# A two-layer decoder trunk: the first and last pairs of tiles of each feed-forward reordered, operands queued among products, and the mixer's last heads beside its first outputs

## The chip, the cores and the metric

The kernel runs on one core of one Trainium2 chip. The metric is device time in microseconds (us); three runs of the kernel before are shown.

## The reference, cut to what matters

Two layers, 512 positions, width 1024, everything in fp32. `ada` is an RMS norm whose scale and shift, like the gates, come from a linear map of `silu(c)`.

```
mod = silu(c) @ w_ada[layer] + b_ada[layer]          # (3 sub-blocks, shift/scale/gate, 1024)
x = x + 0.5 * gate0 * swiglu(ada(x, 0), w1[layer, 0], w2[layer, 0])
x = x + gate1 * mixer(ada(x, 1))                     # q|k|v heads + short conv, then @ w_out
x = x + 0.5 * gate2 * swiglu(ada(x, 2), w1[layer, 1], w2[layer, 1])
# swiglu(h): g, up = split(h @ w1); (silu(g) * up) @ w2, inner width 2816
# mixer: 8 heads of 64, a causal softmax over keys at three dilations; conv: gb * conv3(gc * u)
```

## The kernel before, in words

**Products.** Each fp32 product is three passes of TensorE (PE) over operands that are split into a high and a low half: high by high, high by low, low by high (`product` L273 to L275, `shared_bulk` L280). A weight tile of 128 by 1024 that has landed in `raw`, `left` or `sum` is split by `halves`: ScalarE (ACT) writes `whi` (L167), VectorE (DVE) writes `wlo` (L168). The activations are kept split as `h`.

**Order of the work.** A layer is a feed-forward (FFN), the mixer, and a second FFN; so there are four FFNs and two mixers. The order of all weight units is written out by `_units`, and inside an FFN by `_ffn_order`. `weights` takes them in that order; `fetch` loads them some units ahead (SyncE's queue, SP) and splits them two ahead (`AHEAD`).

**The FFN's first product** is made with seven products of half-size blocks in place of eight. Its 2816 inner columns are 11 pairs of tiles, n = 0 to 10; each pair has seven units of 24 matmuls (128x256), called n.1 to n.7 below. Unit 1 is block b11 in a `left` tile (three buffers). Unit 2 is b12 and unit 4 is b22, in `raw` tiles (five buffers). Unit 5 is b21 + b22 in a `sum` tile (two buffers): SP loads b21, and a GpSimd (POOL) accumulate-DMA adds b22 to it (`add_block`, L179). Unit 6 is that `sum` with b11 taken off (L218), unit 7 is `left` after another accumulate-DMA of b21, which is issued after L218. Unit 3 is b12 less the sum (L221), after which the `sum` buffer is free for the next pair but one. The moving operands of units 1 and 2 are made by `Blocks.early`, those of the others by `t1` to `t4`. After units 7 and 3, `evacuation` makes the hidden tiles `hidh`, `hidl` from the banks.

**The second product** is made in three parts (`PARTS`: pairs 0 to 3, 4 to 7, 8 to 10), P0 and P1 among the units, P2 at the end. `Tail.run` makes one: for each of eight output tiles j, one unit of w2 and its matmuls of 128x512, then the addition into `x` (L526). In P2 the first two j run `side_by_side`, with the last two of their products after the others, and the last three j are run in two halves of 256 columns, so that the norm behind them can start on the first half.

**Queued steps.** `after(columns, step)` puts a step on a list that `tick` works off as PE's products go by; `flush` runs what is left at once. The modulations of later sub-blocks are jobs (`later`: one 128x1024 multiply-and-sum on DVE, L299, after a load of 512 KB); `next_job` gives them out after units 7 and 3 and between the j of P0 and P1. The kernel before gives 61, 26, 52 and 0 of them to the four FFNs.

**The mixer** makes four groups of heads and four groups of convolution, `MIXER`; the attention steps of a group (`attend`: transposes of p L807, products with v L816) are queued among the products of the next. At the end the last group's steps are flushed, the eight y are split into a new `h`, and `Tail.run` makes the output product.

Of the kernel before, what the change touches and what calls it, by code (L numbers as in the profile page):

```python
# [19 lines left out]
S = 512  # L20
# [20 lines left out]
LATER = 2048  # L41

# [44 lines left out]
def _ffn_order():  # L87


    order = [[(0, 1), (0, 2)], [(1, 1), (1, 2)], [(2, 1)], [(2, 2)]]  # L90
    order += [[u] for u in ((0, 5), (1, 5), (0, 6), (1, 6), (0, 7), (2, 5), (0, 4), (0, 3), (1, 7), (2, 6), (1, 4),
                            (1, 3), (3, 1), (2, 7), (3, 2), (2, 4), (2, 3))]
    ends = [p0 + n - 1 for p0, n in PARTS]
    for n in range(3, NP):
        order += [[(n, 5)], [(n, 6)]]
        if n - 1 in ends:
            order += [[("part", ends.index(n - 1))]]
        for p, q in ((1, 7), (2, 4)):
            if n + 1 < NP:
                order += [[(n + 1, p)]]  # L100
            order += [[(n, q)]]
        order += [[(n, 3)]]
    return order + [[("part", len(PARTS) - 1)]]
# [3 lines left out]
def trunk(ctx: ExitStack, tc: tile.TileContext, t: dict):  # L107
# [16 lines left out]
    def half_kb(name):  # L124
        return tmp.tile([128, S], F32, name=name, tag="ev", bufs=7)
# [209 lines left out]
    def later(l, s):  # L335
# [177 lines left out]
    class Tail:  # L513
# [18 lines left out]
        def run(self, ks, key, done, pool=None, side_by_side=0):  # L532
# [4 lines left out]
            n = len(ks)  # L537
# [13 lines left out]
            if side_by_side:  # L551
                banks = [acc_bank() for _ in range(2)]
                for j in range(2):
                    ws[j] = weights(*key, j)
                    products(banks[j], j, slice(0, S), range(n - side_by_side))
                for j in range(2):
                    products(banks[j], j, slice(0, S), range(n - side_by_side, n))
                    self.add(j, banks[j], slice(0, S), done)
                j0 = 2
            for j in range(j0, full):  # L560
                ws[j] = weights(*key, j)
                part(j, slice(0, S))
                if not done:
                    next_job(2)
# [16 lines left out]
            def change(half, rb):  # L581
                for j in range(KD):
                    modulate(h, self.nl, self.ns, rb, HALVES[half], j)

            r = None
            for cols in HALVES:
# [4 lines left out]
                if r:  # L591
                    flush()
                    if blocks:
                        for k in range(KD // 2):
                            blocks.early(r[1], k)
                    else:
                        change(0, r[1])
                r = norm(cols)
            if blocks:
# [6 lines left out]
            elif not self.last:  # L606
                after(0, lambda: change(1, r[1]))
# [80 lines left out]
    def ffn(l, s, h, carried, groups=()):  # L688
# [16 lines left out]
        for at, group in enumerate(todo):  # L705
            if group[0][0] != "part":
                feed(l, which, h, group, banks, done)
                if group[0][1] in (7, 3):

                    left = len(jobs) - 2 * KD * sum(g[0][0] == "part" and g[0][1] < len(PARTS) - 1 for g in todo[at:])  # L710
# [18 lines left out]
    def mixer(l, s, h):  # L729
# [13 lines left out]
        with tc.tile_pool(name="mix", bufs=1) as mp:  # L743
            y = {}

            def project(g):

                ws = [weights("qkv", l, g, u) for u in range(4)]
                qk, v = [], []
                for pair in ((0, 1), (2, 3)):  # L750
                    if g == 0 and pair[0]:
                        flush()
                    banks = [acc_bank()[:, :384] for _ in pair]
                    for k in range(KD):
                        o = (k % 2) * 384
                        for b, ps in zip(pair, banks):
                            tb = slice(b * 128, (b + 1) * 128)
                            bulk(ps, (hh[k][:, tb], hl[k][:, tb]), [w[:, o:o + 384] for w in ws[k // 2]],
                                 k == 0, k == KD - 1)
                    ss = tmp.tile([128, 8], F32, name="sm", tag="sm", bufs=24)  # L760
                    raw = []
                    for i, ps in enumerate(banks):
                        sq = mp.tile([128, 256], F32, name="qq", tag="qq", bufs=2)
                        nc.scalar.activation(sq, ps[:, 0:256], AF.Square)
                        nc.vector.reduce_sum(ss[:, 4 * i:4 * i + 4], sq.rearrange("p (a h) -> p a h", h=HD), axis=AX.X)

                        vt = spare_part("v", 256).rearrange("p (i m h) -> p i m h", i=2, m=2)
                        split(vt[:, :, 0], vt[:, :, 1], ps[:, 256:384].rearrange("p (i h) -> p i h", h=HD))
                        v.append(vt)
                        qn = mp.tile([128, 256], F32, name="qn", tag="qn", bufs=3).rearrange("p (a h) -> p a h", h=HD)  # L770
                        nc.vector.tensor_tensor(out=qn, in0=ps[:, 0:256].rearrange("p (a h) -> p a h", h=HD),
                                                in1=qkg[:, l], op=ALU.mult)
                        raw.append(qn)
                    r = rsqrt(ss, 8, 1.0 / HD)
                    for i, qn in enumerate(raw):
                        nc.vector.tensor_tensor(out=qn, in0=qn, op=ALU.mult,
                                                in1=r[:, 4 * i:4 * i + 4, None].to_broadcast([128, 4, HD]))

                        qt = mp.tile([128, 6, 2, HD], F32R, name="qk", tag="qk", bufs=4)
                        split(qt[:, 0:2, 0], qt[:, 0:2, 1], qn[:, 0:2])  # L780
                        split(qt[:, 2:4], qt[:, 4:6], qn[:, 2:4, None, :].to_broadcast([128, 2, 2, HD]))
                        qk.append(qt)
                return qk, v

            def attend(g, qk, v):

                y[g] = mp.tile([128, S], F32, name="ya", tag="y", bufs=8)
                stacks = [[None] * 3 for _ in range(2)]
                probs, moved = {}, {}

                def lift(i, n):
                    stacks[i][n] = stack(qk, i + 2 * n)

                def soften(b, i):
                    probs[b, i] = softmax(b, stacks[i])

                def turn(b, i):
                    half = b // 2
                    if b % 2 == 0:

                        moved[half, i] = [mp.tile([128, 4, 256], F32R, name=n, tag=n, bufs=2) for n in ("ph", "pl")]
                        for z in moved[half, i]:
                            nc.gpsimd.memset(z[:, 2 * half + 1, 0:128].bitcast(F32), 0.0)
                    p = probs.pop((b, i))
                    pt = tp_bank()
# [238 lines left out]
```

## Time and the profile before

| | |
|---|---|
| median of three runs | 1974.92 us (1971.2 to 1977.33) |
| profiled execution | 1973.8 us, its span 1971.7 us |
| mean granted TensorE clock | 0.976 |
| PE busy | 1864.1 us, 95% |
| PEld (weight loads) busy | 1724.1 us, 87% |
| DVE busy | 1441.7 us, 73% |
| ACT busy | 948.0 us, 48% |
| POOL busy | 88.5 us, 4% |

The profiled execution lies 1.1 us below the median. A clock of 1.0 stands for 2.4 GHz and 0.5 for 1.2 GHz; 0.976 is a mean over the span. Matmuls overlap, so what tells most is PE's idle time and what ended it.

### The profile page before, as it was taken

Reading aid. Unit: us, or ns where it says so; the run is one execution under the profiler, and the core shown is the slowest. Engines: PE = TensorE matmul, PEld = TensorE weight load, DVE = VectorE, ACT = ScalarE, POOL = GpSimd, SP = SyncE. Lnnn points to the kernel's source line nnn. Section 1 sums busy time; section 2 is a strip of 40 time slices with the busy share of each in tenths; the row PEclk is TensorE's granted clock in tenths of the full one; section 3 lists DMA queues with packets and bytes.
Section 4 is the critical chain, followed back from the end, with each engine's and each line's share of the span. In section 5 each row is a group of like instructions: output and inputs, shape, how many; then the busy total and the mean of one; then the engine's idle time right before and its main releaser. Section 6 shows DMA issues by size and latency. Waiting matters only on the chain. (4 is left out here: it accounts for less than half of the span.)

```text
span 1971.7 us, 31053 instructions
## 1 busy us (share of the span) xinstructions
PE 1864.1 (95%) x12340; PEld 1724.1 (87%) x12340; DVE 1441.7 (73%) x2458; ACT 948.0 (48%) x1483; POOL 88.5 (4%) x164
## 2 busy tenths in 40 slices
PE   4899899999999799999988999999999998999998
PEld 3798898899978798998887989898898798989898
DVE  7897878787865777775677878786977767747563
ACT  4552543446653562543464536343655654536342
POOL 0100000000000000000000000000000000000000
PEclk9899999999999899999998999999999998999999
DMA  8778776421314368674507777843222407626422
GB/s 332 185 236 271 209 234 211 142 81 60 108 65 128 70 168 255 180 206 145 152 23 192 234 247 203 273 122 98 81 70 97 143 18 171 167 85 165 131 57 83
DMA packets 86277, 300.52 MB, mean 152 GB/s; under 512 B 9458, under 2 KB 10482, under 8 KB 86132
## 3 DMA queue, kind: packets, MB, share of 16 engines
q1 hardware_dynamic: 73460, 252.40, 37.4%
q0 software_dynamic: 12672, 46.14, 13.8%
q8 instruction: 97, 1.59, 0.3%
q14 instruction: 48, 0.39, 0.1%
HBM read 296.41 MB, written 2.10 MB: 151 GB/s over the span
## 5 line engine op out<-in xcount | busy, mean ns | idle before, releaser
L280 PE MATMUL acc<-h,whi 128*128 128x256 f32 x4928 | 912.0, 287 | 49.0 <-ACT whi L167 22.6
L280 PEld LDWEIGHTS acc<-h,whi 128*128 128x128 f32 x4928 | 783.7, 195 | 58.0 <-ACT whi L167 24.7
L280 PE MATMUL acc<-h,wlo 128*128 128x256 f32 x2464 | 705.2, 287 | 14.9 <-DVE wlo L168 14.9
L280 PEld LDWEIGHTS acc<-h,wlo 128*128 128x128 f32 x2464 | 479.6, 195 | 18.5 <-DVE wlo L168 18.5
L167 ACT ACTIVATE whi<-raw 128x1024 fp32r<-128x1024 f32 (+1 forms) x300 | 302.9, 1012 | 387.0 <-PE acc L274 227.0
L168 DVE TENSOR_TENSOR wlo<-raw,whi 128x1024 fp32r<-128x1024 f32 (+1 forms) x300 | 347.7, 1164 | 60.2 <-ACT whi L167 56.6
L273 PE MATMUL acc<-hidh,whi 128*128 128x512 f32 (+1 forms) x776 | 287.4, 370 | 10.6 <-ACT whi L167 10.6
L274 PE MATMUL acc<-hidl,whi 128*128 128x512 f32 (+1 forms) x776 | 287.3, 370 | 0.0
L275 PE MATMUL acc<-hidh,wlo 128*128 128x512 f32 (+1 forms) x776 | 287.0, 370 | 0.0
L299 DVE SCALAR_TENSOR_TENSOR ada<-ada,cb 128x1024 f32<-128x1024 f32 x144 | 174.4, 1222 | 72.6 <-DMA ada<-in_w_ada 72.2
L526 DVE SCALAR_TENSOR_TENSOR x<-acc,fin,x 128x512 f32<-128x512 f32 (+1 forms) x130 | 87.7, 675 | 143.4 <-PE acc L275 143.0
L167 ACT ACTIVATE whi<-sum 128x1024 fp32r<-128x1024 f32 x88 | 93.3, 1060 | 177.4 <-DVE sum L218 99.2
L273 PEld LDWEIGHTS acc<-hidh,whi 128*128 128x128 f32 x776 | 146.2, 188 | 35.6 <-ACT whi L167 11.4
L274 PEld LDWEIGHTS acc<-hidl,whi 128*128 128x128 f32 x776 | 146.2, 188 | 25.9 <-DVE hidl L510 1.6
L275 PEld LDWEIGHTS acc<-hidh,wlo 128*128 128x128 f32 x776 | 146.2, 188 | 24.6
L167 ACT ACTIVATE whi<-left 128x1024 fp32r<-128x1024 f32 x88 | 93.0, 1056 | 142.0 <-DMA left<-in_w 70.1
L168 DVE TENSOR_TENSOR wlo<-sum,whi 128x1024 fp32r<-128x1024 f32 x88 | 107.5, 1221 | 71.7 <-ACT whi L167 71.7
L168 DVE TENSOR_TENSOR wlo<-left,whi 128x1024 fp32r<-128x1024 f32 x88 | 107.4, 1221 | 56.8 <-ACT whi L167 55.7
L273 PE MATMUL acc<-h,whi 128*128 128x512 f32 (+1 forms) x368 | 139.1, 379 | 0.0
L275 PE MATMUL acc<-h,wlo 128*128 128x512 f32 (+1 forms) x368 | 134.6, 366 | 0.0
L274 PE MATMUL acc<-h,whi 128*128 128x512 f32 (+1 forms) x368 | 134.1, 364 | 0.0
L621 DVE TENSOR_TENSOR ev<-acc,ev 128x512 f32<-128x512 f32 x132 | 90.4, 685 | 3.7 <-PE acc L280 3.0
(115 smaller groups left out, 2159.0 us busy)
## 6 DMA issues: line engine op xcount, KB each, us to landing
ada<-in_w_ada SPq DMA_DIRECT2D x128, 512.0 KB, 4.3
raw<-in_w SPq DMA_DIRECT2D x88, 512.0 KB, 4.4
raw<-in_w2a SPq DMA_DIRECT2D x64, 512.0 KB, 4.8
left<-in_w SPq DMA_DIRECT2D x44, 512.0 KB, 4.6
sum<-in_w SPq DMA_DIRECT2D x44, 512.0 KB, 4.7
sum<-in_w POOLq DMA_DIRECT2D x44, 512.0 KB, 7.3
left<-in_w POOLq DMA_DIRECT2D x44, 512.0 KB, 5.4
raw<-in_w2b SPq DMA_DIRECT2D x32, 384.0 KB, 3.5
```

The lines of the kernel that those rows point to most:

```text
L167: nc.scalar.activation(hi, raw, AF.Copy)
L168: nc.vector.tensor_tensor(out=lo, in0=raw, in1=hi.bitcast(F32), op=ALU.subtract)
L273: nc.tensor.matmul(out, a[0], b[0], start=first, stop=False)
L274: nc.tensor.matmul(out, a[0], b[1], start=False, stop=False)
L275: nc.tensor.matmul(out, a[1], b[0], start=False, stop=last)
L280: nc.tensor.matmul(out, p, q, start=first and i == 0, stop=i == 2, skip_group_check=True)
L299: nc.vector.scalar_tensor_tensor(w, w, 1.0, cb, op0=ALU.mult, op1=ALU.mult, accum_out=raw[:, m, j:j + 1])
L526: nc.vector.scalar_tensor_tensor(x[j][:, cols], ps, gate, x[j][:, cols], op0=ALU.mult, op1=ALU.add)
L621: nc.vector.tensor_tensor(out=v, in0=bank, in1=v, op=ALU.add)
```

## The change

It has six parts.

1. `_ffn_order`: pairs 0 and 1 are brought to their end before pair 2's unit 5 starts (before, pairs 0, 1 and 2 were mixed). At the other end, pairs 9 and 10 are mixed (before, pair 10 stood alone).
2. The `ev` tag has eight buffers for seven, and the space for descriptors of software DMAs is 1024 for 2048.
3. The jobs are 52, 52, 35 and 0 for the four FFNs; in P0 and P1 one is given out before each j and one after each but the last, where there were two after each.
4. Between sub-blocks, the modulation or `early` steps of the first half are queued (`EARLY` = 128 columns apart) among the products of the second half; before, they came after all of them. In front of an FFN the second half's `spread` comes after fewer columns.
5. The mixer's y are split into the old `h` in place. The last group's attention steps and the split of its y (`last_heads`) run among the first two outputs, which take seven of their eight products first.
6. At the start the first modulation tile is loaded ahead of `x`, and its two jobs run ahead of the squares.

```diff
+EARLY = 128
...
-    order += [[u] for u in ((0, 5), (1, 5), (0, 6), (1, 6), (0, 7), (2, 5), (0, 4), (0, 3), (1, 7), (2, 6), (1, 4),
...
+    order += [[u] for u in ((0, 5), (1, 5), (0, 6), (1, 6), (0, 7), (1, 7), (0, 4), (0, 3), (1, 4), (1, 3))]
...
-        return tmp.tile([128, S], F32, name=name, tag="ev", bufs=7)
+        return tmp.tile([128, S], F32, name=name, tag="ev", bufs=8)
...
         if s == 0:
+            gate(l, 0 if l == 0 else 1)
             if l == 0:
-                gate(0, 0)
-            norm(l, 1)
-            gate(l, 1)
+                norm(l, 1)
+                gate(l, 1)
             norm(l, 2)
+            if l > 0:
+                gate(l, 2)
+        elif l + 1 < DEPTH:
             gate(l, 2)
-        elif l + 1 < DEPTH:
             norm(l + 1, 0)
             gate(l + 1, 0)
+            norm(l + 1, 1)
...
+                if late:
+                    ks.append(late())
                 for j in range(2):
                     products(banks[j], j, slice(0, S), range(n - side_by_side, n))
                     self.add(j, banks[j], slice(0, S), done)
+                if then:
+                    then()
                 j0 = 2
             for j in range(j0, full):
+                if not done:
+                    next_job()
                 ws[j] = weights(*key, j)
                 part(j, slice(0, S))
-                if not done:
-                    next_job(2)
+                if not done and j < KD - 1:
+                    next_job()
...
-                after(ROOTED, lambda: r.append(spread(r[0])))
+                after(SUMMED if blocks and cols.start else ROOTED, lambda: r.append(spread(r[0])))
...
-                if r:
-                    flush()
-                    if blocks:
-                        for k in range(KD // 2):
-                            blocks.early(r[1], k)
-                    else:
-                        change(0, r[1])
+                flush()
                 r = norm(cols)
+                if cols.start:
+                    continue
+                if blocks:
+                    for k in range(KD // 2):
+                        after(EARLY, lambda k=k, r=r: blocks.early(r[1], k))
+                else:
+                    change(0, r)
...
+        yh, yl = hh, hl
+        yh[0], yl[0] = [tmp.tile([128, S], F32R, name="y0", tag="ev", bufs=8) for _ in range(2)]
...
+        def last_heads():
             flush()
-            ks = []
-            yh, yl = plain(new_h())
-            for i, k in enumerate((4, 5, 6, 7, 0, 1, 2, 3)):
-                split(yh[i], yl[i], y[k])
-                ks.append((yh[i], yl[i]))
...
+            return halved(KD - 1, 3)
...
+        return tail.run(ks, ("out", l), True, lambda: (op[0], first_tiles(op[0])), 1, last_heads, room), stack
...
-    nc = bacc.Bacc("TRN2", target_bir_lowering=False, num_devices=1, dynamic_dma_scratch_size=2048)
+    nc = bacc.Bacc("TRN2", target_bir_lowering=False, num_devices=1, dynamic_dma_scratch_size=1024)
```

**ACT at the opening of the first FFN**, from unit 0.7's `whi<-left`. The first `whi<-sum` that follows is unit 2.5. Before:

```order
L167 ACTIVATE whi<-left 128x1024
L617 ACTIVATE ev<-ev 128x512
L509 ACTIVATE h<-t 128x2x256 x2
L626 ACTIVATE ev<-acc 128x512
L167 ACTIVATE whi<-sum 128x1024
```

After the change, from the row behind 0.7's (L638 is L626 of before, L629 is L617, L512 is L509):

```order
L629 ACTIVATE ev<-ev 128x512
L167 ACTIVATE whi<-left 128x1024
L512 ACTIVATE h<-t 128x2x256 x2
L167 ACTIVATE whi<-raw 128x1024
L638 ACTIVATE ev<-acc 128x512
L167 ACTIVATE whi<-raw 128x1024
L638 ACTIVATE ev<-acc 128x512
L167 ACTIVATE whi<-raw 128x1024
L638 ACTIVATE ev<-acc 128x512
L167 ACTIVATE whi<-raw 128x1024
L638 ACTIVATE ev<-acc 128x512
L167 ACTIVATE whi<-sum 128x1024
```

Units 1.7 (`left`), 0.4, 0.3, 1.4 and 1.3 (`raw`) now stand ahead of 2.5; before, 2.5 was the next split after 0.7.

**PE at the end of the first FFN.** L280 are units of the first product and L273 to L275 products of P2; `whi_3363` is the weight of unit 10.6, `whi_3401` that of 10.7. Before:

```order
L280 MATMUL acc_3233<-h_186,wlo_3364 128x256
L280 MATMUL acc_3233<-h_186,whi_3363 128x256 x2
L280 MATMUL acc_3233<-h_186,wlo_3364 128x256
L273 MATMUL acc_3570<-hidh_3118,whi_3498 128x512
L274 MATMUL acc_3570<-hidl_3119,whi_3498 128x512
L280 MATMUL acc_3233<-h_185,whi_3401 128x256 x2
L280 MATMUL acc_3233<-h_185,wlo_3402 128x256
L280 MATMUL acc_3233<-h_185,whi_3401 128x256 x2
```

After the change, the last matmuls of unit 10.3 (`whi_3435`) and what follows:

```order
L280 MATMUL acc_3306<-h_190,wlo_3436 128x256
L280 MATMUL acc_3306<-h_190,whi_3435 128x256 x2
L280 MATMUL acc_3306<-h_190,wlo_3436 128x256
L273 MATMUL acc_3544<-hidh_3092,whi_3472 128x512
L274 MATMUL acc_3544<-hidl_3093,whi_3472 128x512
L275 MATMUL acc_3544<-hidh_3092,wlo_3473 128x512
L273 MATMUL acc_3544<-hidh_3092,whi_3472 128x512
```

Before, two matmuls of P2's first output stood between units 10.6 and 10.7, and PE takes its instructions in order; now P2 begins behind the last unit.

**PE where the first layer's mixer ends.** L807 and L816 (L821 and L830 after the change) are the last heads' transposes and their products with v; L273 to L275 are here the last convolution and the outputs. Before:

```order
L273 MATMUL acc<-h,whi 128x512
L274 MATMUL acc<-h,whi 128x512
L275 MATMUL acc<-h,wlo 128x512
L807 MATMUL tp<-ident,p 128x128 x14
L816 MATMUL acc<-ph,h 128x256 x2
L273 MATMUL acc<-h,whi 128x512
L274 MATMUL acc<-h,whi 128x512
L816 MATMUL acc<-pl,h 128x256
L816 MATMUL acc<-ph,h 128x256
L816 MATMUL acc<-pl,h 128x256
```

After the change:

```order
L273 MATMUL acc<-h,whi 128x512
L274 MATMUL acc<-h,whi 128x512
L275 MATMUL acc<-h,wlo 128x512
L821 MATMUL tp<-ident,p 128x128 x4
L273 MATMUL acc<-h,whi 128x512
L821 MATMUL tp<-ident,p 128x128 x4
L274 MATMUL acc<-h,whi 128x512
L275 MATMUL acc<-h,wlo 128x512
L273 MATMUL acc<-h,whi 128x512
L274 MATMUL acc<-h,whi 128x512
L275 MATMUL acc<-h,wlo 128x512
L830 MATMUL acc<-ph,h 128x256
```

Fourteen transposes in a row stood behind the last convolution; now they stand in groups between products of the first two outputs.

## Rows read from the trace of the kernel before

**Rows 1.** The cores of the execution: its span and its mean granted TensorE clock.

```profile
core 0: 1971.7 us, clock 0.976
```

**Rows 2.** The waits of PE over the whole span: line, releaser, us in all, times, longest.

```profile
PE acc L280 <- ACT whi L167: 22.6, 9, 5.5
...
PE acc L273 <- ACT whi L167: 10.6, 4, 2.8
```

**Rows 3.** Timeline 67 to 84 us, first FFN: start, duration, instruction, idle before, releaser.

```profile
67.48 1.22 DVE L221 TENSOR_TENSOR raw<-raw,sum 128x1024 f32<-128x1024 f32 x1
...
68.77 6.21 SPq L194 DMA_DIRECT2D sum<-in_w  x2
...
74.49 0.86 POOL L179 DMA_DIRECT2D sum<-in_w  x1 [7.86 <-DMA sum<-in_w]
...
81.99 1.06 ACT L167 ACTIVATE whi<-sum 128x1024 fp32r<-128x1024 f32 x1 [10.33 <-DMA sum<-in_w]
...
83.10 0.79 PE L280 MATMUL acc<-h,whi 128*128 128x256 f32 x2 [4.15 <-ACT whi L167]
```

**Rows 4.** Timeline of PE, third unit 5 of the other three FFNs.

```profile
690.89 0.80 PE L280 MATMUL acc<-h,whi 128*128 128x256 f32 x2 [5.50 <-ACT whi L167]
...
1058.65 0.80 PE L280 MATMUL acc<-h,whi 128*128 128x256 f32 x2 [4.22 <-ACT whi L167]
...
1652.68 0.79 PE L280 MATMUL acc<-h,whi 128*128 128x256 f32 x2 [2.62 <-ACT whi L167]
```

**Rows 5.** Stretches: bounds, length, busy time of PE, PEld, DVE, ACT, POOL; PEclk; DMA share; GB/s.

```profile
44.30:1971.70 1927.40, 1845.84 (x12280) 1710.30 (x12279) 1407.79 (x2388) 926.98 (x1451) 88.26 (x160) 0.98 0.51 149
81.90:88.70 6.80, 5.13 (x22) 4.84 (x23) 5.58 (x6) 4.87 (x6) 0.86 (x1) 0.50 0.62 109
126.30:129.70 3.40, 3.40 (x17) 3.40 (x17) 1.49 (x2) 1.02 (x2) 0.00 (x0) 0.50 0.86 242
590.50:597.30 6.80, 6.40 (x22) 5.63 (x23) 5.24 (x9) 3.59 (x7) 0.00 (x0) 0.50 0.00 0
```

**Rows 6.** Timeline of ACT and PE where the first FFN ends.

```profile
360.30 1.06 ACT L167 ACTIVATE whi<-left 128x1024 fp32r<-128x1024 f32 x1 [4.53 <-DMA left<-in_w]
...
366.13 0.83 ACT L167 ACTIVATE whi<-raw 128x768 fp32r<-128x768 f32 x1
...
367.01 0.50 PE L273 MATMUL acc<-hidh,whi 128*128 128x512 f32 x1 [2.82 <-ACT whi L167]
```

**Rows 7.** The same view of stretches, from 123 us, second products of the first FFN.

```profile
123.40:225.00 101.60, 94.50 (x583) 85.53 (x583) 79.42 (x106) 39.81 (x49) 4.92 (x6) 0.97 0.77 236
```

**Rows 8.** Timeline of DVE and PE behind the first part.

```profile
206.32 1.23 DVE L299 SCALAR_TENSOR_TENSOR ada<-ada,cb 128x1024 f32<-128x1024 f32 x1 [1.14 <-DMA ada<-in_w_ada]
...
210.49 0.51 PE L280 MATMUL acc<-h,whi 128*128 128x256 f32 x2 [3.53 <-DVE ev L621]
```

**Rows 9.** The waits of PE inside the third FFN, 1104 to 1329 us.

```profile
PE acc L280 <- ACT ev L626: 0.3, 1, 0.3
```

**Rows 10.** Timeline of PE where the mixer's heads end, both layers.

```profile
589.29 1.12 PE L807 MATMUL tp<-ident,p 128*128 128x128 f32 x8 [1.77 <-DVE pl L510]
...
1552.94 1.12 PE L807 MATMUL tp<-ident,p 128*128 128x128 f32 x8 [1.77 <-DVE pl L510]
```

**Rows 11.** Timeline of PE between the mixer and the second FFN.

```profile
642.73 0.58 PE L401 MATMUL tp<-ones,ssq 128*128 128x1 f32 x4 [1.63 <-DVE ssq L395]
644.49 1.31 PE L280 MATMUL acc<-h,whi 128*128 128x256 f32 x5 [1.18 <-ACT h L509]
```

**Rows 12.** The view of stretches, second FFN's opening and the steady first FFN.

```profile
653.90:681.70 27.80, 23.87 (x173) 22.90 (x173) 27.51 (x40) 19.55 (x32) 1.73 (x2) 0.88 0.30 59
230.00:270.00 40.00, 40.00 (x342) 40.00 (x341) 33.68 (x41) 23.50 (x30) 3.47 (x4) 1.00 0.77 212
```

**Rows 13.** DMA issues of the page: tile, queue, number, size, median us to landing.

```profile
ada<-in_w_ada SPq DMA_DIRECT2D x128, 512.0 KB, 4.3
...
sum<-in_w POOLq DMA_DIRECT2D x44, 512.0 KB, 7.3
```

More of the change, by code (lines that the diff above doesn't have):

```diff
@@ L530, in add, with run @@
                 squares(self.acc, j, cols)
-        def run(self, ks, key, done, pool=None, side_by_side=0):
+        def run(self, ks, key, done, pool=None, side_by_side=0, late=None, then=None):
             ws = {}
-            n = len(ks)
+            n = len(ks) + (late is not None)
             def products(ps, j, cols, which):
@@ L606, in run @@
             elif not self.last:
-                after(0, lambda: change(1, r[1]))
+                change(1, r)
             return h
@@ L708, in ffn @@
                 if group[0][1] in (7, 3):
-                    left = len(jobs) - 2 * KD * sum(g[0][0] == "part" and g[0][1] < len(PARTS) - 1 for g in todo[at:])
+                    left = len(jobs) - (2 * KD - 1) * sum(g[0][0] == "part" and g[0][1] < len(PARTS) - 1 for g in todo[at:])
                     places = sum(g[0][1] in (7, 3) for g in todo[at:])
@@ new lines, in mixer, with halved @@
+        for kind, n in MIXER:
+            if kind == "heads":
+                attend(n, *project(n))
+            else:
+                conv(n)
+        while finished < {0, 1, 2}:
+            steps.pop(0)[1]()
+        ks = []
+        yh, yl = hh, hl
+        yh[0], yl[0] = [tmp.tile([128, S], F32R, name="y0", tag="ev", bufs=8) for _ in range(2)]
+        def halved(i, k):
+            split(yh[i], yl[i], y[k])
+            return yh[i], yl[i]
+        for i, k in enumerate((4, 5, 6, 7, 0, 1, 2)):
+            ks.append(halved(i, k))
@@ L896, in first_tiles, with room @@
+        stack = ExitStack()
+        op = []
+        def last_heads():
+            flush()
+            return halved(KD - 1, 3)
+        def room():
+            mix.close()
+            open_sums()
+            op.append(stack.enter_context(tc.tile_pool(name="out", bufs=1)))
+            for j in range(KD - SPLIT, KD):
+                place["out", l, j] = op[0], SPLIT
+        return tail.run(ks, ("out", l), True, lambda: (op[0], first_tiles(op[0])), 1, last_heads, room), stack
     def first_tiles(pool):
@@ L923, in trunk @@
             nc.sync.dma_start(par, t["par"])
-    load_ada()
     load_ada()
@@ L932, in trunk @@
         nc.scalar.activation(cb[:, cols], ps, AF.Silu)
+    for m in range(2):
+        ada_job(ada[0][:, m], 0, 0, m, 0)
     acc = sums()
@@ L935, in trunk @@
         squares(acc, j, slice(0, S))
+    load_ada()
     load_ada()
@@ L946, in side_by_side @@
             for j in (2 * k, 2 * k + 1):
-                for m in range(2):
+                for m in range(2) if j else ():
                     ada_job(ada[j][:, m], 0, 0, m, j)
-                if len(ada) < KD:
+                if j and len(ada) < KD:
                     load_ada()
```

265 lines of the change are left out of this document (128 added, 137 removed).

## The prediction

> **What bounds the kernel now.** I began with the cores and the page's busy times. PE is busy in 1864.1 of 1971.7 us, so nothing but PE can be the bound, and the change takes no product away: its worth lies in PE's idle time and in PE's clock. The mean granted clock is 0.976 [rows 1], so 0.024 x 1971.7 = 47.3 us are the price of stretches at 1.2 GHz. Without the first 44 us the kernel still shows 0.98 and 1927.40 - 1845.84 = 81.6 us of idle PE [rows 5].
>
> Next came the waits of PE: it waits longest for whi, 22.6 us in nine waits in front of the FFN's units (the longest 5.5), and 10.6 us in four waits in front of w2's products [rows 2]. The timeline shows where these stand, and the view of stretches what the clock does behind them. Every stretch at 1.2 GHz is 3.4 or 6.8 us long and begins during or shortly after a wait of PE: 81.9 to 88.7 has 0.50 around the wait that ends at 83.10, 126.3 to 129.7 follows waits at 123 to 126, and 590.5 to 597.3 follows one that ends at 589.29 [rows 3, 5, 10]. In a stretch at half clock, half of PE's busy time is lost. So a wait costs its idle time plus 1.7 us (3.40 / 2) or 2.6 us (5.13 / 2) of slow products.
>
> **Pair 2's sum tile, four times.** The chain in the first FFN [rows 3]: L221 of pair 0 ends at 67.48 + 1.22 = 68.70 and frees one of two `sum` buffers; SP starts b21 at 68.77; POOL starts the accumulate-DMA at 74.49; ACT splits at 81.99; PE starts at 83.10 after 4.15 us idle. Nothing in the new order makes that chain shorter, as pair 0's unit 6 stays where it was. What moves is the need: units 1.7, 0.4, 0.3, 1.4 and 1.3 now stand ahead of 2.5. A unit takes 24 x 40.00 / 342 = 2.81 us of PE [rows 12], five take 14.0, and the longest of the four waits is 5.50 [rows 4]. So the tile is there some 8 us or more ahead of its need. The idle time is 4.15 + 5.50 + 4.22 + 2.62 = 16.5 us [rows 3, 4], and each place has a 6.8 us stretch at half clock, 4 x 2.57 = 10.3 [rows 5]. Together **26.8**. If only the idle time comes back it is 16.5.
>
> The Trainium skill (Perfetto Trace Analysis, Identifying Performance Opportunities) says that a gap which repeats on the engine that should be full can mean too little SBUF for the next tile to be allocated. By that rule only a third `sum` buffer would help, the change adds none, and the 26.8 us fall out of the sum. The trace agrees that the buffer is what is waited for, but this gap stands once per FFN, not once per pair.
>
> **The end of the FFN, four times.** Two products of P2 stand ahead of unit 10.7. Unit 10.7's whi is made at 360.30 to 361.36, but w2's whi starts only at 366.13, and PE is idle for 2.82 us until 367.01 [rows 6], with 10.7 ready behind it. The four are 10.6 us [rows 2]; behind three of them PE runs a 3.4 us stretch at half clock like the one at 126.3 [rows 5], 3 x 1.7 = 5.1. In the new order P2 begins behind the last unit, and the last two pairs alternate, so each evacuation has another unit to lie beside. Together **15.7**. Price if the cover fails: unit 10.3's own evacuation (ACT, then DVE) is late before P2's last products, at most the same 2.8 us each.
>
> **Jobs in the first FFN.** From 123.4 to 225.0 PE is idle 101.60 - 94.50 = 7.1 us [rows 7], and two stretches at half clock follow (3.4). The longest wait: the last two jobs of P0 wait for their own loads on DVE (1.14 us idle before 206.32), the wlo of the next units and L621 queue behind them, and PE waits 3.53 us at 210.49 [rows 8]. With 61 - 32 = 29 jobs for 21 places behind units 7 and 3 there are two jobs at eight places; with 52 - 30 = 22 for 20 at two only, and P0's last output has none behind it. The third FFN shows what remains: its 52 - 32 = 20 jobs stand at one per place, and PE waits 0.3 us there from 1104 to 1329 [rows 9]. Together **10.5**, all of it.
>
> **Last heads.** PE waits 1.77 us for `pl` in either layer [rows 10], and behind the first 6.40 us of products run at half clock [rows 5], a loss of 3.2. Now those steps lie among two outputs. What replaces them: the eighth operand (y of group 3) and its split must be ready after 7 + 7 products; I allow 1.0 us of new waits per layer, between 0 and the old 1.77. Together 4.0 + 0.8 = **4.8**.
>
> **From the mixer to the next FFN, twice.** PE waits 1.63 us for the sums and 1.18 us for the first operand [rows 11]; a 3.4 us stretch at half clock (1.7) follows. Now the first half's operands are made beside the second half's outputs, so the first product starts directly: at most 1.63 + 1.18 + 1.7 = 4.5 per layer. But DVE is busy 27.51 of the 27.80 us behind that [rows 12]: PE gains there only what DVE starts earlier, and the small waits inside that stretch may grow. Bounds 2.8 and 4.5; I take 4.0, since DVE starts as much earlier as PE. Together **8.0**.
>
> **At nothing.** The start: a tile of 1 MB ahead of `x` delays the squares by no more than one load's 4.3 us [rows 13] and takes two jobs of 1.23 us [rows 8] out of what follows; 0, between 1.8 lost and 2.5 won. The eighth `ev` buffer and the norm steps inside a layer: the work beside them is products that PE has anyway; 0 to 1. New waits: unit 1.7 now follows 0.7 directly and needs its accumulate-DMA earlier, 0 to 1.5 per FFN, taken as 0.5; and the second FFN now has 22 jobs at those places where it had none, 0 to 7.1 (the first FFN's price), taken as 1, because the third FFN bears the same load [rows 9]. That is **3.0** to lose.
>
> **Sum.** 26.8 + 15.7 + 10.5 + 4.8 + 8.0 - 3.0 = 62.8 us. Against the profiled execution: 1973.8 - 62.8 = 1911.0. The median of before lies 1.1 us above that execution, so the forecast is **1912**.
>
> **Rivals.**
> - *The clock does not come back.* Of the sum, 10.3 + 5.1 + 3.4 + 3.2 + 3.4 = 25.4 us are clock. If half-clock stretches are granted elsewhere instead (small waits remain where DVE is the limit), 37.4 us are left: 1937. For it: such stretches stand in the opening from 653.9 to 681.7 too, mean clock 0.88, with only 3.9 us of idle PE [rows 12]. Against it: in the stretch from 230 to 270 without waits the clock is 1.00.
> - *More clock than counted.* 47.3 - 25.4 = 21.9 us of clock are lost in stretches that I left alone [rows 1]; if most go as well, some 1893.
> - *The gap at pair 2 only moves*, to pair 3's sum, as there are still two buffers: 26.8 less, 1939. For it: the chain from L221 to the split is as long as before, 13.3 us [rows 3]. Against it: the other buffer is freed by pair 1's unit 6, one unit later, and pair 3's sum is needed only after all of pair 2.
> - *Slower: software DMAs in single file.* The space for descriptors is halved. If the second of POOL's two adds of a pair could only start when the first has landed, a pair would need at most 2 x (0.86 + 7.3) = 16.3 us [rows 3, 13] against 7 x 2.81 = 19.7 us of PE [rows 12], which hides it. It decides where the two adds pass 19.7 + 62.8 / 44 = 21.1 us, as then 44 pairs lose what the change wins: an add would have to land in 9.7 us for 7.3. At 12 us, 44 x (25.7 - 19.7) = 264 are lost, 2176. For it: nothing in the trace shows how much of the space an add takes. Against it: at the landing time that the rows show, even single file is hidden.
> - *No change at all*, were all moved waits to come back at the next unit: 1975.
>
> The Trainium skill (DMA: Bandwidth & Descriptors, SWDGE vs HWDGE vs iDMA) has the software queue's descriptor rings in a carved-out part of SBUF, and this is the part that the change halves. No run so far shows how much of it these adds use.
>
> **How the numbers follow.** My sum's case, 1900 to 1925, 0.60. Clock not back, 1928 to 1940, 0.18. More clock, 1890 to 1900, 0.07. The gap moves, 1935 to 1942, 0.07. No change, 0.03; slower, 0.05. About 0.3% (6 us) is what a measurement of this kernel tells from nothing, so faster has 0.92, same 0.03, slower 0.05. The range reaches over the first three cases: 1893 to 1940; outside it are no change, slower, and part of the moved gap and the fastest.
>
> **What would show it.** Right: no PE wait above 1 us for whi in front of a unit 5, and no 6.8 us stretch at half clock there; PE's waits of L273 for whi (10.6 us) gone; from 123 to 225 us under 1 us of waits; mean clock 0.985 or more. Wrong: the same waits for `sum` at pair 3, POOL's landing times well above 7.3 us, DVE-released waits in the second FFN, or a clock that stays near 0.976 while idle PE falls.

## The result, and the profile after

The changed kernel takes 1904.92 us (median of four runs, 1903.16 to 1905.65); the kernel before takes 1975.63 us in runs beside it. The ratio is 0.9644, 95% interval 0.9627 to 0.9661: 70.7 us or 3.6% less. The forecast was 1912, in a range from 1893 to 1940. The profiled execution took 1905.03 us, 68.8 less than that of before.

The cores of the changed kernel: span and mean granted clock, beside [rows 1].

```profile
core 0: 1903.2 us, clock 0.991
```

By the mean clock, the stretches at 1.2 GHz now stand for 0.009 x 1903.2 = 17.1 us, where they stood for 47.3. That also counts the time in which PE is idle inside them. Counted as the prediction counts a stretch, as half of PE's busy time in it, the stretches behind the first 44 us cost 43.0 us before (20 of them) and 14.5 now (six): 28.5 us came from the clock. PE's idle time over the whole span went from 1971.7 - 1864.1 = 107.6 to 1903.2 - 1832.5 = 70.7 us, 36.9 less. The other 3.1 us of the 68.6 by which the span is shorter are busy time outside the slow stretches, and no run gives a place for them. The page of the changed kernel:

```profile
PE 1832.5 (96%) x12340; PEld 1699.7 (89%) x12340; DVE 1442.6 (76%) x2458; ACT 944.2 (50%) x1482; POOL 88.5 (5%) x164
```

The view of stretches (columns as in [rows 5]): the kernel without its first 44 us, the first FFN's P0 with the units around it, and three of the six stretches at half clock that are left ahead of the final stores.

```profile
44.30:1903.20 1858.90, 1813.56 (x12273) 1685.21 (x12271) 1407.89 (x2388) 923.40 (x1450) 88.34 (x160) 0.99 0.52 154
113.00:215.00 102.00, 100.31 (x674) 92.59 (x673) 80.74 (x106) 43.59 (x53) 5.21 (x6) 1.00 0.78 233
73.80:80.60 6.80, 5.92 (x26) 5.63 (x27) 6.16 (x6) 0.69 (x3) 0.72 (x1) 0.50 0.76 200
643.90:650.70 6.80, 5.40 (x25) 5.40 (x26) 6.80 (x9) 3.15 (x4) 0.86 (x1) 0.50 0.55 94
974.90:981.70 6.80, 4.82 (x22) 4.82 (x23) 5.85 (x13) 5.69 (x13) 0.00 (x0) 0.50 0.00 0
```

Idle PE behind the first 44 us went from 81.6 to 1858.90 - 1813.56 = 45.3 us. From 113 to 215 us, which holds what [rows 7] held, it went from 7.1 to 1.7; that is one wait of 1.69 us for `ev`. PE's waits, beside [rows 2]:

```profile
PE acc L280 <- ACT h L512: 18.5, 7, 5.3
PE acc L280 <- ACT ev L638: 10.4, 7, 3.4
PE acc L280 <- DVE wlo L168: 9.5, 5, 3.1
...
PE acc L280 <- ACT whi L167: 3.4, 2, 1.7
```

The waits of L273 for `whi` (10.6 us) are gone, and those of L280 for `whi` fell from 22.6 to 3.4. In their place stands a kind that was small: 10.4 us for `ev` L638, the copy of a PSUM bank by ACT, in seven waits, for 1.9 in three before. The 18.5 us for `h` were there before (19.3), and 15.4 of them lie in the first 60 us. P2's first product follows unit 10.3 with no idle time noted, where [rows 6] had 2.82 us:

```profile
358.70 0.40 PE L273 MATMUL acc<-hidh,whi 128*128 128x512 f32 x1
```

PE's timeline at the places where it still waits, beside [rows 3, 4, 8]:

```profile
74.36 0.80 PE L280 MATMUL acc<-h,whi 128*128 128x256 f32 x2 [3.42 <-ACT ev L638]
...
641.75 0.50 PE L280 MATMUL acc<-h,whi 128*128 128x256 f32 x2 [1.72 <-ACT whi L167]
645.30 0.58 PE L280 MATMUL acc<-h,wlo 128*128 128x256 f32 x1 [3.05 <-DVE wlo L168]
...
703.49 0.50 PE L280 MATMUL acc<-h,whi 128*128 128x256 f32 x2 [2.28 <-ACT ev L638]
...
910.57 0.50 PE L280 MATMUL acc<-h,whi 128*128 128x256 f32 x2 [0.98 <-ACT ev L638]
...
926.27 0.50 PE L280 MATMUL acc<-h,whi 128*128 128x256 f32 x2 [1.30 <-ACT ev L638]
```

None of these is pair 2's unit 5. The ones at 641.75 and 645.30 are for units 0.6 and 1.5, in a stretch in which VectorE is the limit (busy 27.75 of 28.00 us from 628 to 656), and one of the half-clock stretches shown above stands around the second (643.90 to 650.70). The wait of 2.28 us at 703.49 has no slow stretch behind it here; in the next execution of the same kernel (below) it is 2.36 us and has one:

```profile
703.30:706.70 3.40, 3.40 (x18) 3.40 (x17) 2.88 (x4) 0.49 (x1) 0.00 (x0) 0.50 1.00 402
```

### The profile page after: what moved, and what is told of

The parts are those of the page before. It is cut to its first block, busy times and chain, and to the rows that moved or that the text cites. A ratio compares the mean times of both kernels' runs of the same rounds, so it can differ in the third digit from the quotient of the medians.

```text
span 1903.2 us, 31033 instructions
## 1 busy us (share of the span) xinstructions
PE 1832.5 (96%) x12340; PEld 1699.7 (89%) x12340; DVE 1442.6 (76%) x2458; ACT 944.2 (50%) x1482; POOL 88.5 (5%) x164
## 4 chain that ended last, share of the span: by engine, by line
PE 56%; DVE 3%; ACT 2%; DMA 1%; issue 1%; ACTq 0%; POOLq 0%
PE acc L280 27%; PE acc L273 9%; PE acc L274 9%; PE acc L275 9%; DMA left<-in_w 1%; ACT whi L167 1%; DVE h L513 1%; PE acc L830 0%; DVE wlo L168 0%; PE tp L821 0%; PE tp L851 0%; ACT tv L455 0%; ACT ev L638 0%; ACT h L512 0%; DVE sum L218 0%
## 5 line engine op out<-in xcount | busy, mean ns | idle before, releaser
L280 PE MATMUL acc<-h,whi 128*128 128x256 f32 x4928 | 891.6, 283 | 35.0 <-ACT h L512 18.5
L280 PEld LDWEIGHTS acc<-h,whi 128*128 128x128 f32 x4928 | 766.9, 191 | 41.1 <-ACT h L512 21.8
L280 PE MATMUL acc<-h,wlo 128*128 128x256 f32 x2464 | 694.2, 282 | 9.7 <-DVE wlo L168 9.5
L280 PEld LDWEIGHTS acc<-h,wlo 128*128 128x128 f32 x2464 | 470.2, 191 | 11.2 <-DVE wlo L168 11.2
L273 PE MATMUL acc<-hidh,whi 128*128 128x512 f32 (+1 forms) x776 | 287.1, 370 | 0.0
L275 PE MATMUL acc<-hidh,wlo 128*128 128x512 f32 (+1 forms) x776 | 286.7, 369 | 0.0
L275 PEld LDWEIGHTS acc<-hidh,wlo 128*128 128x128 f32 x776 | 146.2, 188 | 24.9
L273 PEld LDWEIGHTS acc<-hidh,whi 128*128 128x128 f32 x776 | 146.2, 188 | 24.3
L273 PE MATMUL acc<-h,whi 128*128 128x512 f32 (+1 forms) x346 | 132.0, 382 | 0.4 <-ACT h L512 0.4
L274 PE MATMUL acc<-h,whi 128*128 128x512 f32 (+1 forms) x346 | 126.8, 366 | 1.0 <-DVE h L513 1.0
L275 PE MATMUL acc<-h,wlo 128*128 128x512 f32 (+1 forms) x346 | 127.0, 367 | 0.0
L273 PE MATMUL acc<-whi,h 128*128 128x384 f32 x256 | 88.9, 349 | 4.9 <-ACT h L436 4.9
```

What stands on the lines that cost most here:

```text
L273: nc.tensor.matmul(out, a[0], b[0], start=first, stop=False)
L274: nc.tensor.matmul(out, a[0], b[1], start=False, stop=False)
L275: nc.tensor.matmul(out, a[1], b[0], start=False, stop=last)
L280: nc.tensor.matmul(out, p, q, start=first and i == 0, stop=i == 2, skip_group_check=True)
```

## Where the time came from

For this table I took from both timelines the end of the last matmul of the same unit, at the borders of the stages, and compared the distances. F1 to F4 are the four FFNs. "Opening" reaches to the end of unit 5.3 in F1 and 3.3 in the others, and holds the start of the FFN behind a mixer; "end" reaches from P1's to P2's last product. The forecast's terms are put in the stage where they fall.

| stage | before, from to (us) | after, from to (us) | less by | forecast |
|---|---|---|---|---|
| F1 opening with P0 | 25.55 to 235.84 | 24.84 to 222.02 | 13.1 | 16.7 |
| F2 opening, from the mixer's end | 641.09 to 747.73 | 618.26 to 715.06 | 9.8 | 10.6 |
| F3 opening | 1011.63 to 1116.50 | 976.88 to 1072.69 | 9.1 | 6.3 |
| F4 opening, from the mixer's end | 1602.69 to 1709.87 | 1552.08 to 1646.23 | 13.0 | 8.7 |
| F1 end | 324.61 to 410.15 | 310.81 to 392.69 | 3.7 | 2.8 |
| F2 end | 919.64 to 1006.41 | 886.98 to 971.66 | 2.1 | 4.2 |
| F3 end | 1288.42 to 1375.37 | 1244.61 to 1326.49 | 5.1 | 4.4 |
| F4 end | 1881.79 to 1968.14 | 1818.14 to 1899.59 | 4.9 | 4.2 |
| first mixer: last convolution to second output | 586.87 to 607.09 | 568.08 to 583.86 | 4.4 | 4.0 |
| second mixer, the same | 1550.51 to 1568.27 | 1501.91 to 1517.68 | 2.0 | 0.8 |
| all else | | | 1.4 | 0 |
| sum | | | 68.6 | 62.8 |

A stage is not the same in every execution. The first FFN's opening takes 210.3 us here and 213.3 in another run with the same code in that FFN (the last pairs alone); with the changed code it takes 197.2 here and 195.9 to 199.8 in five more runs. So a difference of 2 or 3 us in that row tells nothing.

## The experiments

Parts were put alone into the kernel before, or taken alone out of the changed kernel. The sixth part (the start) and the earlier `spread` of the fourth had no run of their own. Ratios are to the kernel before, run beside each group (medians 1976.7 to 1977.9), and what is less than before is worked out from the ratio.

**The opening order alone.**

```diff
-    order += [[u] for u in ((0, 5), (1, 5), (0, 6), (1, 6), (0, 7), (2, 5), (0, 4), (0, 3), (1, 7), (2, 6), (1, 4),
-                            (1, 3), (3, 1), (2, 7), (3, 2), (2, 4), (2, 3))]
+    order += [[u] for u in ((0, 5), (1, 5), (0, 6), (1, 6), (0, 7), (1, 7), (0, 4), (0, 3), (1, 4), (1, 3))]
...
-    for n in range(3, NP):
+    for n in range(2, NP):
...
```

The two buffers' sizes of part 2, which this order needs, are in this run too; alone they change nothing (below).

> The kernel before with the new opening order of the feed-forwards alone (pairs 0 and 1 ended before pair 2's unit 5) and the eighth ev buffer with the smaller software-DMA space that this order needs. My theory (the need of pair 2's sum moves past the chain that makes it): four waits of 4.15, 5.50, 4.22 and 2.62 us and four stretches at half clock go, 26.8 us less, about 1949 beside 1975.6. If the clock does not come back: 16.5 less, 1959. If the gap only moves to pair 3's sum, as there are still two buffers: within 3 us of before, with PE waiting for whi of a sum in each opening.

Measured: 1949.67 us, ratio 0.9856 (0.9830 to 0.9882), 28.5 us less. PE's waits (line numbers here are one lower):

```profile
PE acc L272 <- ACT whi L166: 11.1, 4, 2.9
PE acc L279 <- ACT ev L625: 9.8, 4, 3.7
PE acc L279 <- ACT whi L166: 4.3, 3, 1.8
```

The waits in front of units fall to 4.3 us from 22.6, while those of the FFN's end (L272) stay. Neither rival holds. But the order has a price: 9.8 us of waits for the copy `ev`, 3.7 of them in the first FFN, which the changed kernel shows as well.

**The last pairs alone.**

```diff
-    for n in range(3, NP):
+    for n in range(3, NP - 2):
...
+    order += [[u] for u in ((n, 5), (n, 6), (m, 1), (n, 7), (m, 2), (m, 5), (m, 6), (n, 4), (m, 7), (n, 3), (m, 4),
+                            (m, 3))]
```

> The kernel before with the new order of the last two pairs alone (9 and 10 mixed). My theory: the four waits of P2's first products for their whi (10.6 us) and three stretches of 3.4 us at half clock (5.1) go, 15.7 us less, about 1960; mean clock up by about 0.0025. If the clock does not come back: 10.6 less, 1965. If the wait moves to the evacuation of the last unit in front of P2: no change beyond 3 us, with PE waits for hidh or hidl at P2.

Measured: 1953.25 us (1947.74 to 1958.5), ratio 0.9873 (0.9847 to 0.9899), 25 us less, more than each theory said. The profiled execution is the longest of the four, at 1958.5. Its four ends, by the steps of the table, are shorter by 3.7, 4.9, 5.1 and 4.9 us, 18.5 together; the first FFN's opening, untouched by the edit, was 3.0 longer than in before's profile. What is shown is the 18.5; the other 6 or so lie in the spread of the runs, and I can give no place for them.

**The jobs alone**: the `later` and `next_job` lines of the change.

> The kernel before with the jobs redistributed alone (52, 52, 35, 0 for 61, 26, 52, 0; one before each output of P0 and P1 and one behind each but the last). My theory: the first feed-forward's waits between 123 and 225 us (7.1) and the two stretches at half clock behind them (3.4) go, and the second feed-forward loses about 1: 9 to 10 us less, about 1966. Rival (the jobs were only placed beside those waits, which come from the order of the first pairs): at most 3 us less. Rival (VectorE of the second feed-forward over PE's pace): up to 7 us of waits there, so 3 less in all or none.

Measured: 1963.9 us, ratio 0.9937 (0.9915 to 0.9959), 12.5 less. By the steps, the first FFN up to unit 5.3 is 10.0 us shorter, so the first rival falls: its wait behind P0 (3.53 us, [rows 8]) is gone, and from 107 to 226 us PE waits once.

```profile
PE acc L280 <- ACT ev L631: 1.3, 1, 1.3
```

The second rival holds in part: from unit 1.3 to 3.3 the second FFN is 5.8 us longer, with these waits of PE, and a stretch at half clock behind the second:

```profile
714.93 0.51 PE L280 MATMUL acc<-h,whi 128*128 128x256 f32 x2 [1.31 <-ACT ev L631]
...
731.80 0.55 PE L280 MATMUL acc<-h,whi 128*128 128x256 f32 x2 [2.66 <-ACT ev L631]
```

**A third sum buffer, in the old order.**

```diff
-            b["sum"] = sum_pool[0].tile([128, 1024], F32, name="sum", tag="sum", bufs=2)
+            b["sum"] = sum_pool[0].tile([128, 1024], F32, name="sum", tag="sum", bufs=2 if pair[1:3] == (0, 0) else 3)
...
```

> The kernel before, its order untouched, with a third sum buffer from the second feed-forward on (the first has room for two only). It leaves out the attention's mask (other numbers stand in its place, and it isn't loaded) and halves the software-DMA space, to make room. If the buffer is what the sum of pair 2 waits for: the waits of 5.50, 4.22 and 2.62 us in feed-forwards 2 to 4 go with their three stretches at half clock, 12.3 + 7.7 = 20 us less, about 1956, and the wait of 4.15 us in the first stays. If the chain of loads itself is late whatever the buffers (SyncE's queue, landing times): no change beyond 3 us.

Measured: 1946.65 us, ratio 0.9841 (0.9822 to 0.9860), 31 less, more than the 20 expected. PE's timeline, at the first FFN's pair 2 (two buffers still) and in the second FFN's opening (three):

```profile
83.05 0.79 PE L279 MATMUL acc<-h,whi 128*128 128x256 f32 x2 [4.03 <-ACT whi L166]
...
671.27 0.51 PE L279 MATMUL acc<-h,whi 128*128 128x256 f32 x2 [1.84 <-ACT whi L166]
672.41 0.58 PE L279 MATMUL acc<-h,wlo 128*128 128x256 f32 x1 [0.63 <-DVE wlo L167]
...
678.23 0.50 PE L279 MATMUL acc<-h,whi 128*128 128x256 f32 x2 [1.28 <-ACT whi L166]
679.50 0.58 PE L279 MATMUL acc<-h,wlo 128*128 128x256 f32 x1 [0.76 <-DVE wlo L167]
```

The wait of 4 us in the first FFN stays; the one of 5.50 us in the second is gone, and only the small early ones remain. So the buffer is what the sum waited for, and the chain of loads is early enough once it has one. From their first matmul to unit 3.3, FFNs 2 to 4 are 6.6, 8.0 and 11.8 us shorter here; with the new order alone 6.3, 7.3 and 7.7. So the order does what a third buffer of 4 KB per partition does, for which this run had to leave out the mask.

**The changed kernel once more**, as the standard for the next three.

> The changed kernel once more, as the standard for the three that run beside it on the same chip. All theories: a ratio of about 0.964 to the kernel before, some 1905 us.

Measured: 1904.27 us, ratio 0.9636 (0.9612 to 0.9661).

**The last heads ahead of the outputs**, in the changed kernel.

```diff
-        return tail.run(ks, ("out", l), True, lambda: (op[0], first_tiles(op[0])), 1, last_heads, room), stack
+        ks.append(last_heads())
+        return tail.run(ks, ("out", l), True, lambda: (op[0], first_tiles(op[0])), 1, None, room), stack
```

> The changed kernel with the last heads undone: their steps are flushed and the y of group 3 is split ahead of the first two outputs, all else as changed. My theory: PE waits again for pl in both layers (1.77 us each) and a stretch at half clock can follow, 4.8 us slower than the changed kernel (1.8 at least, without the clock), and the second output of the first layer ends 3 to 4.5 us later than in the changed kernel. Rival (the wait was only moved, and y of group 3 is late for the eighth product either way): within 1 us of the changed kernel.

Measured: 1916.0 us, ratio 0.9694 (0.9670 to 0.9718), 11.7 more than the changed kernel. From the last convolution to the second output it takes 6.9 and 6.5 us more. The wait for `pl` comes back, longer than in [rows 10]:

```profile
574.48 1.75 PE L821 MATMUL tp<-ident,p 128*128 128x128 f32 x7 [4.57 <-DVE pl L513]
```

A stretch of 6.8 us at half clock stands around it (574.1 to 581.0). The second layer has the same wait of 4.57 us, and a stretch from 1512.8 to 1519.6. The mechanism is shown. Its size here is no measure of the old order's, since the seven splits of y stand ahead of the last heads' steps on DVE in this kernel, and behind them in the kernel before.

**The first half's operands not queued**, in the changed kernel.

```diff
-                flush()
+                if r:
+                    flush()
+                    if blocks:
+                        for k in range(KD // 2):
+                            blocks.early(r[1], k)
...
                 r = norm(cols)
-                if cols.start:
-                    continue
...
```

> The changed kernel with the first half's norm and early steps put back behind all products of the second half, as before the change, all else as changed. My theory: the waits of 1.63 us for ssq and 1.18 us for the first operand between mixer and feed-forward come back in both layers, with their stretches at half clock: 4 us per layer, 8 us slower than the changed kernel. Rival (VectorE's opening stretch sets the time there, whatever PE does first): PE starts 3 us later but pair 1 ends at the same distance from the mixer's end, within 2 us of the changed kernel in all.

Measured: 1909.15 us (1901.9 to 1913.39), ratio 0.9659 (0.9633 to 0.9684), 4.9 more than the changed kernel, between theory and rival. The intervals overlap (0.9612 to 0.9661 for the changed kernel), so this total is only a rough size; the trace shows the mechanism. The old waits are back in full:

```profile
623.03 0.58 PE L404 MATMUL tp<-ones,ssq 128*128 128x1 f32 x4 [1.64 <-DVE ssq L398]
624.79 1.11 PE L280 MATMUL acc<-h,whi 128*128 128x256 f32 x5 [1.18 <-ACT h L512]
```

The FFN behind the first mixer starts 3.05 us later, but pair 1 ends only 2.6 later, and 2.4 behind the second (2.8 and 2.6 beside the repeat of the changed kernel). Between the two FFNs, not queueing is 1.8 us better up to the end of pair 1. Each mixer takes 1.4 us more up to its last convolution in this kernel, with a stretch at half clock at its start, which the queued order has in neither.

**The jobs in another split**, in the changed kernel.

```diff
-            gate(l, 0 if l == 0 else 1)
...
+            norm(l, 1)
+            gate(l, 1)
...
-                    next_job()
+                    next_job(2 if j == 2 else 1)
...
```

> The changed kernel with its jobs given out 52, 35, 52, 0 (the second feed-forward spared, the third as in the kernel before), 16 in each of P0 and P1 and so one per place, eight before P0 where a gate is needed there. The trace of the changed kernel shows waits of 2.28, 0.98 and 1.30 us in the second feed-forward, each behind a VectorE or ScalarE queue with jobs in it. If its 52 jobs cause them: about 5 us less than the changed kernel, 1900, and pair 3 ends 39.6 us behind pair 1 there, for 42.1. If the new order of the units causes them: no change beyond 1.5 us; if they only move with the jobs, waits of the same size in the third feed-forward.

Measured: 1904.17 us, ratio 0.9639 (0.9615 to 0.9664), no change. The second FFN's end is 2.8 us shorter and has no wait left, so what stood there was the jobs' doing (in the repeat of the changed kernel only 1.1 us stand there). Its wait near pair 3 stayed (43.4 us from 1.3 to 3.3, for 42.1 and, in the repeat, 43.8), but eight jobs stand ahead of P0 there in either kernel; the opening order alone, with no jobs there, takes 39.6. The first FFN grew by 4.4 us, with 16 jobs in each part for 15; in the last run below it grew by 2.6 with no edit in it.

**Waits made on purpose**, in the changed kernel.

```diff
+                if group == [(6, 7)]:
+                    for _ in range((7, 9, 11, 14)[2 * l + which]):
+                        nc.vector.tensor_tensor(out=cb, in0=cb, in1=cb, op=ALU.max)
```

> The changed kernel with idle work on VectorE ahead of a unit in the middle of each feed-forward (pair 6, where PE waits for nothing now): 7, 9, 11 and 14 copies of a 128x1024 tile onto itself. They hold up the next wlo and so PE, longer in each feed-forward. My theory (a wait costs its idle time and a stretch at half clock behind it): no wait or a short one without such a stretch in the first; in the last two, idle time and a stretch of 3.4 or 6.8 us at clock 0.5 right behind it, so that pair 8 ends later by the idle time plus 1.7 to 3.4 us. Rival (the stretches come at times of their own, not from waits): pair 8 ends later by the idle time alone, and the stretches of the run stand where they do in the changed kernel.

Measured: 1931.71 us, ratio 0.9770 (0.9746 to 0.9794). The doses did not come out as meant: the third FFN got several waits, the fourth none, so it tells nothing. In the first a wait without a stretch was expected, and it came with one. PE's timeline in the first three, and the stretches behind those waits:

```profile
246.84 0.58 PE L280 MATMUL acc<-h,wlo 128*128 128x256 f32 x1 [1.99 <-DVE wlo L168]
...
832.28 0.80 PE L280 MATMUL acc<-h,whi 128*128 128x256 f32 x2 [5.71 <-ACT whi L167]
...
1149.63 0.51 PE L280 MATMUL acc<-h,whi 128*128 128x256 f32 x2 [2.41 <-DVE ev L633]
...
1164.03 0.50 PE L280 MATMUL acc<-h,whi 128*128 128x256 f32 x2 [2.82 <-ACT ev L638]
...
1279.88 0.50 PE L280 MATMUL acc<-h,whi 128*128 128x256 f32 x2 [2.67 <-DVE ev L633]
```

```profile
246.90:250.30 3.40, 3.40 (x16) 3.40 (x17) 2.76 (x3) 2.02 (x3) 0.00 (x0) 0.50 0.89 245
830.60:837.40 6.80, 5.12 (x24) 5.12 (x25) 4.19 (x6) 1.63 (x2) 0.19 (x1) 0.50 0.68 192
1150.00:1153.40 3.40, 3.40 (x32) 3.40 (x31) 3.37 (x4) 1.48 (x2) 0.32 (x1) 1.00 0.00 0
1165.10:1168.50 3.40, 3.40 (x19) 3.40 (x18) 1.09 (x1) 0.31 (x1) 0.00 (x0) 0.50 0.98 354
1281.10:1284.50 3.40, 3.40 (x18) 3.40 (x18) 3.40 (x5) 2.54 (x4) 0.86 (x1) 0.50 0.43 47
```

The waits of 1.99, 5.71, 2.82 and 2.67 us have a stretch at 0.50 around or right behind them, at places where the changed kernel has none; the one of 2.41 has none behind it (1150 to 1153.4 is at 1.00). From unit 5.3 to 8.3 the second FFN is 9.25 us longer: 5.71 + 0.43 of idle time, 5.12 / 2 = 2.6 of slow products, and 0.5 that I can't place. The rival, that the stretches come at times of their own, falls. Whether a wait near 2.4 us draws one can't be told from its length alone: the same wait in the second FFN of the changed kernel had one in one execution (2.36 us) and none in another (2.28).

**The two buffers' sizes alone.**

```diff
-        return tmp.tile([128, S], F32, name=name, tag="ev", bufs=7)
+        return tmp.tile([128, S], F32, name=name, tag="ev", bufs=8)
...
-    nc = bacc.Bacc("TRN2", target_bir_lowering=False, num_devices=1, dynamic_dma_scratch_size=2048)
+    nc = bacc.Bacc("TRN2", target_bir_lowering=False, num_devices=1, dynamic_dma_scratch_size=1024)
```

> The kernel before with the eighth ev buffer and the smaller space for software DMAs alone. My theory: nothing, within 3 us of before, and the landing time of POOL's adds stays at 7.3 us for a sum. Rival (software DMAs in single file): landing times or the distance between POOL's adds grow, and the time with them, 10 us or more slower.

Measured: 1978.23 us, ratio 1.0005 (0.9991 to 1.0018): nothing. The sum's add lands in 7.3 us here, as in [rows 13], and in the changed kernel in 7.4:

```profile
sum<-in_w POOLq DMA_DIRECT2D x44, 512.0 KB, 7.4
```

**A version made of these readings**: the changed kernel with jobs 52, 35, 52 and 0, and no queueing between two FFNs.

> The changed kernel with two of its steps set otherwise, after what the runs showed: jobs 52, 35, 52, 0 (eight before the second feed-forward's P0 for its gate), and the first half's operands between two feed-forwards behind all products again, where queueing them seemed to cost 1.8 us. If the pieces add: 2.8 us less at the second feed-forward's end and 1.8 less at the third's opening, 4 to 5 us below the changed kernel, 1900. If the jobs' waits only go to the third feed-forward: within 2 us of the changed kernel.

Measured: 1905.56 us, ratio 0.9641 (0.9621 to 0.9661), no better. The second FFN's end is 2.8 us shorter, and the third FFN's first units 2.0; but unit 3.3 comes 2.2 later behind them, so what was won in the opening is given back two pairs on. Neither step alone does that: from 1.3 to 3.3 the third FFN takes 39.6 us with the jobs of the other split and 39.3 with the operands not queued, for 41.8 here, where two jobs stand at each of the first two places. And the first FFN, whose code is the changed kernel's, is 2.6 us longer in this profile, with a wait of 2.43 us for `ev` ahead of P0 and a stretch at half clock behind it. That is spread, and as large as what the steps were to win.

## Why the prediction was right

**The clock and the idle time.** The sum of 62.8 was made of 37.4 us of idle time and 25.4 of clock. Counted the same way, the measured 68.6 hold 36.9 of idle time, 28.5 of clock and 3.1 that no run places. "The clock does not come back" is out: more of the clock came back than was counted. That the idle time agrees is in part luck, since it is made of misses both ways, which follow. The 47.3 us of the rival "more clock than counted" also hold idle time inside the stretches; by PE's busy time the stretches cost 43.0, so 17.6 us of clock were left, not 21.9. What the sum lacked is seen in the fourth FFN's opening, 13.0 for 8.7. The kernel before has two stretches there that I left out of the sum:

```profile
1631.50:1634.90 3.40, 3.21 (x15) 3.21 (x16) 3.40 (x6) 1.15 (x2) 0.86 (x1) 0.51 0.01 2
1638.40:1645.20 6.80, 6.15 (x29) 6.16 (x30) 5.13 (x5) 0.60 (x1) 0.86 (x1) 0.50 0.52 164
```

They cost (3.21 + 6.15) / 2 = 4.7 us. The changed kernel has one of 3.4 us in that opening (1.7), and no other behind it until the final stores; so 3.0 of the 4.3 are clock.

**Pair 2's sum.** Right in mechanism and size: 26.8 forecast, 28.5 with the order alone. The rule of the Trainium skill (Perfetto Trace Analysis, Identifying Performance Opportunities) named the cause, as a third buffer also ends the wait (31 us less). The conclusion that only a buffer would help is not the page's but was drawn in the prediction, and the run with two buffers shows that a later need does it too.

**The FFN's end.** 15.7 forecast, 15.7 measured, but that is luck, two errors that cancel: the order is worth 18.5, and 2.8 are lost again in the second FFN to jobs, as the run without them shows (1.1 in the repeat of the changed kernel).

**The jobs.** "10.5, all of it" was right for the first FFN alone (10.0). The step "the third FFN bears the same load" was wrong for the second, whose loss I took as 1: it was 5.8 in the old order, and in the new one 2.6 near pair 3 (42.1 for 39.6; 4.2 in the repeat) and 2.8 at its end.

**The first FFN's opening** fell short, 13.1 for 16.7, by no more than its spread. But the new wait of 3.42 us at 74.36, with its half-clock stretch (73.80 to 80.60, 5.92 / 2 = 3.0 us), was not foreseen, and every run with the new opening order has it (3.2 to 4.2 us). I had named the accumulate-DMA of unit 1.7 as what might be late; late was the copy of a bank on ACT (L638), behind two splits of weights and some operand casts. The first split had itself waited 2.17 us for PE:

```profile
70.78 1.06 ACT L167 ACTIVATE whi<-left 128x1024 fp32r<-128x1024 f32 x1 [2.17 <-PE acc L280]
71.75 1.13 ACT L512 ACTIVATE h<-t 128x512 fp32r<-128x512 f32 x2
...
72.78 1.04 ACT L167 ACTIVATE whi<-raw 128x1024 fp32r<-128x1024 f32 x1
...
73.73 0.57 ACT L638 ACTIVATE ev<-acc 128x512 f32<-128x512 f32 x1
```

**The last heads** gave 6.4 for 4.8; the new waits were below the 1.0 us that I allowed (none is above 0.5). Of the 6.4, 4.0 come without any slow stretch: with the opening order alone both layers take 17.8 us there and show none, and after the change 15.8. The rest is the first layer's stretch at half clock, 20.2 us in all, which the old order doesn't always have. **Mixer to FFN** was taken too high: each start moved by 3.05 us, and 2.4 to 2.8 of that were kept by pair 1, at or below the lower bound of 2.8; VectorE's full stretch behind it is the likely taker of the rest. **At nothing** were the buffers, rightly: software DMAs in single file, the slower rival, shows nowhere. The start, also at nothing, won 0.7 us (25.55 to 24.84), within its bounds.

Of the signs named ahead, the mean clock (0.991 for 0.985) and the two waits for `whi` came as said. From 113 to 215 us PE is idle for 1.7 us, not under 1, and up to 2.4 in other runs with the same first FFN. One sign of being wrong came too, a wait for DVE in the second FFN: 3.05 us at 645.30, where the longest such wait in a unit was 1.60 before. It stands where VectorE is the limit and did not upset the sum.

## What to carry to other kernels

A wait for a buffer can be ended by the order of the work as well as by another buffer: look for work that is ready and stands behind the waiting instruction, and count how long it lasts. Count a wait of the matrix engine with the slow stretch around it, here about two fifths of all that was won. Then look at what the moved work puts on the queues of the helper engines, since the new waits (PSUM copies behind weight splits) are there.

## What was not expected of the hardware

A wait of 1.99 us was followed by 3.4 us at 1.2 GHz, and one of 2.41 us by none. The same wait of one kernel was followed by such a stretch in one execution and by none in another. The kernel before spread over 16 us between its lowest and highest run (1966.88 to 1983.2 in one group), the changed one over 4 (1902.33 to 1906.57).
